# Rolling a matrix along its rows: the last quarter of the long copies in DMAs of one row per engine, with a window of DMAs in flight

## The chip, the cores and the metric

The kernel runs on one core of a Trainium2 chip. The metric is the device time of one execution in microseconds (us), lower is better; 2% either way counts as a change. Runs were made on several chips, and chips differ by over 1% on this kernel, so kernels are compared only with the runs of the kernel before on the same chip and in the same rounds. All runs here are at a granted clock of 1.0. A ratio is the mean time of one kernel's runs over that of the other's of the same rounds, so it is not quite the ratio of the medians that are quoted beside it.

## The reference

```python
x = np.random.randn(8192, 8192).astype(np.float32)   # 256 MiB
return np.roll(x, 100, axis=1)
```

Nothing is computed. Every byte has to be read once from HBM (the chip's main memory) and written once, 100 columns further right.

## The kernel before

`s` is 100, `a` is 128 and `g` is 28. The columns from 128 on (8,064 floats, 32,256 bytes of each row) are copied from HBM to HBM by DMAs on two rings (queues of DMAs), one issued by SP (`nc.sync`) and one by ACT (`nc.scalar`). The first 128 columns go through SBUF on GpSimd's own queue, with small VectorE copies. The outermost dimension `e` of a DMA has size 16, one value for each of the core's 16 DMA engines; the trace shows 16 increments of the semaphore for each DMA. A DMA has 512 row pieces, so 32 for each engine.

```python
engines = [nc.sync, nc.scalar]
xm = x.rearrange("(c e j) w -> j e c w", e=16, j=4)
om = out.rearrange("(c e j) w -> j e c w", e=16, j=4)
depth = n_rows // 64 // 4                     # 32 rows for each engine
for c in range(4):
    for j in range(4):
        cs = slice(c * depth, (c + 1) * depth)
        engines[j % 2].dma_start(out=om[j, :, cs, a:], in_=xm[j, :, cs, g:n_cols - s])
# ... (GpSimd loads both sides of the first 128 columns, VectorE joins them, GpSimd stores)
for k, h in enumerate(tiles):
    for q in range(Q):
        nc.gpsimd.dma_start(out=ot[k, q, :, :, :a], in_=h[:, q])
```

Of the kernel before, what the change touches and what calls it, by code (L numbers as in the profile page):

```python
# [1 line left out]

# [4 lines left out]


@with_exitstack
def kernel(  # L10
    ctx: ExitStack,
    tc: tile.TileContext,
    x: bass.AP,
    shift: int,
    out: bass.AP,
):
    nc = tc.nc
    n_rows, n_cols = x.shape
    s = shift % n_cols
    a = -(-s // 128) * 128  # L20
    g = a - s
    P = nc.NUM_PARTITIONS
    engines = [nc.sync, nc.scalar]
    n_chunks = 16
    rows = n_rows // n_chunks




    xm = x.rearrange("(c e j) w -> j e c w", e=16, j=4)  # L30
    om = out.rearrange("(c e j) w -> j e c w", e=16, j=4)
    depth = n_rows // 64 // 4
    for c in range(4):
        for j in range(4):
            if a < n_cols:
                cs = slice(c * depth, (c + 1) * depth)
                engines[j % 2].dma_start(out=om[j, :, cs, a:], in_=xm[j, :, cs, g:n_cols - s])
    if a == 0:
        return


    if a > 512:
        for i in range(n_chunks):
            r = slice(i * rows, (i + 1) * rows)
            nc.gpsimd.dma_start(out=out[r, :s], in_=x[r, n_cols - s:])
            if g > 0:
                nc.gpsimd.dma_start(out=out[r, s:a], in_=x[r, :g])
        return





    Q, J = 4, 8
    n_st = n_rows // (P * Q * J)
    reads = ctx.enter_context(tc.tile_pool(name="reads", bufs=n_st))
    heads = ctx.enter_context(tc.tile_pool(name="heads", bufs=n_st))
    xt = x.rearrange("(k p j q) c -> k q p j c", q=Q, j=J, p=P)
    ot = out.rearrange("(k p j q) c -> k q p j c", q=Q, j=J, p=P)
    tiles = []  # L60
    for k in range(n_st):
        t = reads.tile([P, Q - 1, J, a], x.dtype)
        h = heads.tile([P, Q, J, a], x.dtype)
        for q in range(1, Q):
            lead = bass.AP(tensor=x.tensor, offset=(k * P * J * Q + q) * n_cols - s,
                           ap=[[J * Q * n_cols, P], [Q * n_cols, J], [1, a]])
            nc.gpsimd.dma_start(out=t[:, q - 1], in_=lead)  # L67
        nc.gpsimd.dma_start(out=h[:, Q - 1, :, :s], in_=xt[k, Q - 1, :, :, n_cols - s:])  # L68
        nc.vector.tensor_copy(h[:, :Q - 1, :, :s], t[:, :, :, :s])  # L69
        if g > 0:  # L70
            nc.gpsimd.dma_start(out=h[:, 0, :, s:], in_=xt[k, 0, :, :, :g])  # L71
            nc.vector.tensor_copy(h[:, 1:, :, s:], t[:, :, :, s:])  # L72
        tiles.append(h)
    for k, h in enumerate(tiles):
        for q in range(Q):
            nc.gpsimd.dma_start(out=ot[k, q, :, :, :a], in_=h[:, q])  # L76


# [1 line left out]
_INS = ['x', 'shift']  # L80
_OUTS = [((8192, 8192), 'float32')]

_NUMBERS = {'shift': 100}


# [26 lines left out]
```

## Time and profile before

| what | value |
|---|---|
| time, six runs beside the changed kernel | 828.66 us median, 828.28 to 829.5 |
| run that was profiled (most likely on another, faster chip) | 817.2 us, span 815.4 us |
| bytes on the two rings, and on GpSimd's queue | 2 x 132.12 MB, 8.39 MB |
| data rate with the rings alone, 480 to 780 us | 332 GB/s copied, 664 GB/s of HBM traffic |
| last increments of SP's last DMA | first engine 755.8, last engine 813.3 us |

Read the profile from the data side: compute engines are idle, so the page's DMA lines and the table of windows (its last two columns: busy share of the 16 DMA engines, GB/s) tell nearly everything. The prediction below shows the lines.

### The profile page before, as it was taken

The numbers are of one execution on the slowest core, as the hardware profiler recorded it, in microseconds if no ns is written. First come the engines' busy times: TensorE is split into PE (matmuls) and PEld (weight loads), VectorE is DVE, ScalarE is ACT, GpSimd is POOL, SyncE is SP. The second block draws the span as 40 slices with busy tenths as digits, with TensorE's granted clock in tenths as the row PEclk, the third lists the DMA queues.
The fourth block names the chain that finished last, engine by engine and source line by source line (L and its number), as shares of the span: only waits on it lengthen the run. The fifth ranks groups of instructions, "written<-read, shape, count | busy, mean of one in ns | idle before, by whom it ended". The sixth has DMA issues, their size and how long they took to land. (4 is left out here: it accounts for less than half of the span.)

```text
span 815.4 us, 93 instructions
## 1 busy us (share of the span) xinstructions
DVE 3.7 (0%) x4; POOL 16.1 (2%) x22
## 2 busy tenths in 40 slices
DVE  0000000000000000000000000000000000000000
POOL 3000001000010000000000000000000000000000
DMA  9999999999999999999999999999999999999996
GB/s 310 341 328 347 330 349 335 337 340 346 338 337 346 338 348 348 347 333 345 340 344 337 349 326 335 334 329 334 335 329 331 329 335 334 332 331 332 329 334 250
DMA packets 10784, 272.63 MB, mean 334 GB/s; under 512 B 544, under 2 KB 544, under 8 KB 2592
## 3 DMA queue, kind: packets, MB, share of 16 engines
q10 hardware_dynamic: 4224, 132.12, 47.0%
q1 hardware_dynamic: 4224, 132.12, 46.9%
q0 software_dynamic: 2336, 8.39, 4.5%
HBM read 268.44 MB, written 268.44 MB: 658 GB/s over the span
## 5 line engine op out<-in xcount | busy, mean ns | idle before, releaser
L76 POOL DMA_DIRECT2D out_dram<-h x8 | 6.9, 954 | 170.1 <-DMA h<-in_x_dram 144.1
L67 POOL DMA_DIRECT2D t<-in_x_dram x6 | 5.4, 910 | 0.8 <-PEq L107 0.8
L69 DVE COPY h<-t 128x2400 f32<-128x2400 f32 x2 | 2.8, 1410 | 208.5 <-DMA t<-in_x_dram 208.5
L71 POOL DMA_DIRECT2D h<-in_x_dram x2 | 1.8, 883 | 28.6 <-DMA t<-in_x_dram 28.6
L68 POOL DMA_DIRECT2D h<-in_x_dram x2 | 1.8, 882 | 27.0 <-DMA t<-in_x_dram 27.0
L72 DVE COPY h<-t 128x672 f32<-128x672 f32 x2 | 1.0, 503 | 0.0
L93 POOL MEMSET const-float32-0.0<- 128x1 f32 x1 | 0.1, 99 | 0.2 <-issue 0.2
L93 POOL MEMSET const-bfloat16-1.0<- 128x1 bf16 x1 | 0.1, 103 | 0.0
L93 POOL MEMSET const-float32-1.0<- 128x1 f32 x1 | 0.1, 99 | 0.0
L93 POOL MEMSET const-uint8-127<- 128x1 uint8 x1 | 0.1, 99 | 0.0
## 6 DMA issues: line engine op xcount, KB each, us to landing
out_dram<-in_x_dram SPq DMA_DIRECT2D x8, 16128.0 KB, 401.3
out_dram<-in_x_dram ACTq DMA_DIRECT2D x8, 16128.0 KB, 400.5
out_dram<-h POOLq DMA_DIRECT2D x8, 512.0 KB, 182.5
t<-in_x_dram POOLq DMA_DIRECT2D x6, 512.0 KB, 118.2
h<-in_x_dram POOLq DMA_DIRECT2D x2, 400.0 KB, 151.3
h<-in_x_dram POOLq DMA_DIRECT2D x2, 112.0 KB, 146.1
```

Of the source, the lines that this page charges most:

```text
L67: nc.gpsimd.dma_start(out=t[:, q - 1], in_=lead)
L68: nc.gpsimd.dma_start(out=h[:, Q - 1, :, :s], in_=xt[k, Q - 1, :, :, n_cols - s:])
L69: nc.vector.tensor_copy(h[:, :Q - 1, :, :s], t[:, :, :, :s])
L71: nc.gpsimd.dma_start(out=h[:, 0, :, s:], in_=xt[k, 0, :, :, :g])
L72: nc.vector.tensor_copy(h[:, 1:, :, s:], t[:, :, :, s:])
L76: nc.gpsimd.dma_start(out=ot[k, q, :, :, :a], in_=h[:, q])
L93: nc = _bacc.Bacc("TRN2", target_bir_lowering=False, num_devices=1)
```

## The change

Its intent is to let the 16 DMA engines end together. Three quarters of the rows stay in DMAs of 32 rows per engine. The last quarter becomes 64 DMAs for each ring, of one row per engine. A ring issues the next of these only when an older one has landed, that is, when all 16 engines have added one to its semaphore (a counter that engines can wait on). At first 6 may be in flight on a ring, at the end 2. The framework's automatic waits do not allow that, so all DMAs move into a critical section (a stretch of code in which the kernel sets every wait itself) with semaphores of their own, and the GpSimd part is rewritten to match. The core of the diff (the rest rewrites the GpSimd part):

```diff
-    depth = n_rows // 64 // 4
-    for c in range(4):
-        for j in range(4):
-            ...
-                engines[j % 2].dma_start(out=om[j, :, cs, a:], in_=xm[j, :, cs, g:n_cols - s])
+    blocks = n_rows // 64
+    whole = blocks * 3 // 4
+    depth = 32
+    window = 6
...
+    with tc.tile_critical():
...
+        for q, ring in enumerate(rings):
+            bulk = nc.alloc_semaphore(f"bulk{q}")
+            slots = [nc.alloc_semaphore(f"slot{q}_{i}") for i in range(window)]
...
+                for c in range(0, whole, depth):
+                    for j in range(q, 4, 2):
+                        cs = slice(c, min(c + depth, whole))
+                        issue(ring, bulk, om[j, :, cs, a:], xm[j, :, cs, g:n_cols - s])
+                n, left, after = 0, 2 * (blocks - whole), []
+                for c in range(whole, blocks):
+                    for j in range(q, 4, 2):
+                        flying = max(2, window - n * (window - 1) // left)
+                        if n >= flying:
+                            ring.wait_ge(*after[n - flying])
+                        sem = slots[n % window]
+                        issue(ring, sem, om[j, :, c, a:], xm[j, :, c, g:n_cols - s])
+                        after.append((sem, expect[sem]))
+                        n += 1
```

More of the change, by code (lines that the diff above doesn't have):

```diff
@@ L22 @@
     P = nc.NUM_PARTITIONS
-    engines = [nc.sync, nc.scalar]
-    n_chunks = 16
-    rows = n_rows // n_chunks
+    rings = (nc.sync, nc.scalar)
     xm = x.rearrange("(c e j) w -> j e c w", e=16, j=4)
     om = out.rearrange("(c e j) w -> j e c w", e=16, j=4)
-    depth = n_rows // 64 // 4
-    for c in range(4):
-        for j in range(4):
-            if a < n_cols:
-                cs = slice(c * depth, (c + 1) * depth)
-                engines[j % 2].dma_start(out=om[j, :, cs, a:], in_=xm[j, :, cs, g:n_cols - s])
@@ L38 @@
-    if a == 0:
-        return
-    if a > 512:
-        for i in range(n_chunks):
-            r = slice(i * rows, (i + 1) * rows)
-            nc.gpsimd.dma_start(out=out[r, :s], in_=x[r, n_cols - s:])
-            if g > 0:
-                nc.gpsimd.dma_start(out=out[r, s:a], in_=x[r, :g])
-        return
-    Q, J = 4, 8
-    n_st = n_rows // (P * Q * J)
-    reads = ctx.enter_context(tc.tile_pool(name="reads", bufs=n_st))
-    heads = ctx.enter_context(tc.tile_pool(name="heads", bufs=n_st))
@@ L58 @@
-    xt = x.rearrange("(k p j q) c -> k q p j c", q=Q, j=J, p=P)
-    ot = out.rearrange("(k p j q) c -> k q p j c", q=Q, j=J, p=P)
-    tiles = []
-    for k in range(n_st):
-        t = reads.tile([P, Q - 1, J, a], x.dtype)
-        h = heads.tile([P, Q, J, a], x.dtype)
-        for q in range(1, Q):
-            lead = bass.AP(tensor=x.tensor, offset=(k * P * J * Q + q) * n_cols - s,
-                           ap=[[J * Q * n_cols, P], [Q * n_cols, J], [1, a]])
-            nc.gpsimd.dma_start(out=t[:, q - 1], in_=lead)
-        nc.gpsimd.dma_start(out=h[:, Q - 1, :, :s], in_=xt[k, Q - 1, :, :, n_cols - s:])
-        nc.vector.tensor_copy(h[:, :Q - 1, :, :s], t[:, :, :, :s])
-        if g > 0:
-            nc.gpsimd.dma_start(out=h[:, 0, :, s:], in_=xt[k, 0, :, :, :g])
-            nc.vector.tensor_copy(h[:, 1:, :, s:], t[:, :, :, s:])
-        tiles.append(h)
@@ L74 @@
-    for k, h in enumerate(tiles):
-        for q in range(Q):
-            nc.gpsimd.dma_start(out=ot[k, q, :, :, :a], in_=h[:, q])
+    blocks = n_rows // 64
+    whole = blocks * 3 // 4
+    depth = 32
+    window = 6
+    Q, J = 4, 8
+    narrow = 0 < a <= 512
+    n_st = n_rows // (P * Q * J) if narrow else 0
+    pool = ctx.enter_context(tc.tile_pool(name="heads", bufs=1))
+    reads = [pool.tile([P, Q - 1, J, a], x.dtype, name=f"reads{k}") for k in range(n_st)]
+    heads = [pool.tile([P, Q, J, a], x.dtype, name=f"heads{k}") for k in range(n_st)]
@@ new lines, with issue @@
+    with tc.tile_critical():
+        expect = {}
+        def issue(eng, sem, o, i):
+            eng.dma_start(out=o, in_=i).then_inc(sem, 16)
+            expect[sem] = expect.get(sem, 0) + 16
+        for q, ring in enumerate(rings):
+            bulk = nc.alloc_semaphore(f"bulk{q}")
+            slots = [nc.alloc_semaphore(f"slot{q}_{i}") for i in range(window)]
+            if a < n_cols:
+                for c in range(0, whole, depth):
[12 more added lines that the diff above has]
+                        n += 1
+            for sem in (bulk, *slots):
+                if sem in expect:
+                    ring.wait_ge(sem, expect[sem])
+        pooled = nc.gpsimd
+        paired = nc.alloc_semaphore("paired")
+        stored = nc.alloc_semaphore("stored")
+        xt = x.rearrange("(k p j q) c -> k q p j c", q=Q, j=J, p=P)
+        ot = out.rearrange("(k p j q) c -> k q p j c", q=Q, j=J, p=P)
+        n_pair = 0
+        for k in range(n_st):
+            t, h = reads[k], heads[k]
+            landed = nc.alloc_semaphore(f"landed{k}")
+            for q in range(1, Q):
+                lead = bass.AP(tensor=x.tensor, offset=(k * P * J * Q + q) * n_cols - s,
+                               ap=[[J * Q * n_cols, P], [Q * n_cols, J], [1, a]])
+                issue(pooled, landed, t[:, q - 1], lead)
+            issue(pooled, landed, h[:, Q - 1, :, :s], xt[k, Q - 1, :, :, n_cols - s:])
+            if g > 0:
+                issue(pooled, landed, h[:, 0, :, s:], xt[k, 0, :, :, :g])
+            nc.vector.wait_ge(landed, expect[landed])
+            nc.vector.tensor_copy(h[:, :Q - 1, :, :s], t[:, :, :, :s]).then_inc(paired, 1)
+            n_pair += 1
+            if g > 0:
+                nc.vector.tensor_copy(h[:, 1:, :, s:], t[:, :, :, s:]).then_inc(paired, 1)
+                n_pair += 1
+        per = n_pair // n_st if n_st else 0
+        for k in range(n_st):
+            pooled.wait_ge(paired, (k + 1) * per)
+            for q in range(Q):
+                issue(pooled, stored, ot[k, q, :, :, :a], heads[k][:, q])
+        if a > 0 and not narrow:
+            for r in range(0, n_rows, 512):
+                issue(pooled, stored, out[r:r + 512, :s], x[r:r + 512, n_cols - s:])
+                if g > 0:
+                    issue(pooled, stored, out[r:r + 512, s:a], x[r:r + 512, :g])
+        if stored in expect:
+            pooled.wait_ge(stored, expect[stored])
```

## The prediction

> **What bounds the kernel now.** I read the page of the kernel before first, for who is busy at all, then the table of windows, for how the data rate changes with time, and last the ring's waits and the times of the single semaphore increments in the trace.
>
> ```profile
> span 815.4 us, 93 instructions
> ...
> DVE 3.7 (0%) x4; POOL 16.1 (2%) x22
> ...
> DMA  9999999999999999999999999999999999999996
> ...
> q10 hardware_dynamic: 4224, 132.12, 47.0%
> q1 hardware_dynamic: 4224, 132.12, 46.9%
> q0 software_dynamic: 2336, 8.39, 4.5%
> HBM read 268.44 MB, written 268.44 MB: 658 GB/s over the span
> ...
> out_dram<-in_x_dram SPq DMA_DIRECT2D x8, 16128.0 KB, 401.3
> ```
>
> The compute engines do nothing that counts. The DMA engines are nine tenths busy or more in every slice but the last. Two rings (q1 and q10, issued by ACT and SP) move the long row pieces from HBM to HBM, one packet of 32,256 bytes for each row piece (4,096 on each ring, the other 128 packets being semaphore writes), and the GpSimd queue q0 moves the first 128 columns through SBUF. All of it adds up to 658 GB/s of HBM traffic.
>
> ```profile
> 100.00:200.00 100.00, 0.00 (x0) 3.46 (x4) 1.00 1.00 340
> 200.00:440.00 240.00, 1.83 (x2) 3.47 (x4) 1.00 1.00 342
> 480.00:620.00 140.00, 0.00 (x0) 0.00 (x0) 1.00 1.00 332
> 620.00:780.00 160.00, 0.00 (x0) 0.00 (x0) 1.00 0.99 332
> 780.00:790.00 10.00, 0.00 (x0) 0.00 (x0) 1.00 0.95 342
> 790.00:800.00 10.00, 0.00 (x0) 0.00 (x0) 1.00 0.88 319
> 800.00:805.00 5.00, 0.00 (x0) 0.00 (x0) 1.00 0.79 323
> 805.00:810.00 5.00, 0.00 (x0) 0.00 (x0) 1.00 0.66 284
> 810.00:815.40 5.40, 0.00 (x0) 0.00 (x0) 1.00 0.22 96
> ```
>
> In this table of windows the last two columns are the busy share of the 16 DMA engines and the GB/s moved. The fall from 342 to 332 is not a loss. The GpSimd queue's last transfer lands at 462.8 us, so its 8.39 MB ran at 18 GB/s beside some 324 of the rings. A ring byte is read and written in HBM, a GpSimd byte touches HBM once: 2 x 324 + 18 = 666 GB/s before, 2 x 332 = 664 after. So HBM traffic is flat at about 665 GB/s from 100 to 790 us, whatever the mix. That flat rate is the bound. A single engine is not at its own limit meanwhile: in the packet records a row piece takes 1.55 us between 520 and 700 us, but exactly 1.194 us (27.0 GB/s) when others have stopped. At 27 GB/s each, 332 / 27 = 12.3 busy engines are enough to fill the shared rate. From 780 to 800 us with only some 14.8 busy it still held; only after 800 us does it drop.
>
> The last pair of bulk DMAs shows the uneven ends. The sixteen increments of SP's last DMA come at 755.8, 795.9, 799.6, 801.1 and then twelve times between 807.2 and 813.3 us; ACT's last is at 814.4. One engine is done 57 us early, three more about 15 us early, the rest within 6 us.
>
> **What the Trainium skill says.** "HBM Reference", section "Specifications", gives about 716 GB/s for an HBM domain; the 665 measured here is 93% of it, so the trace agrees that one core's DRAM-to-DRAM copy is held by HBM and not by how it is issued. "DMA: Bandwidth & Descriptors", section "Why a DMA increments its semaphore by 16 and not by 1": each engine that takes part counts separately and only the full 16 means landed, so a wait on a DMA is a wait for its slowest engine. The sixteen separate increments above agree. The same section wants one semaphore for each in-flight slot, and the new kernel has six for each ring. Section "Measured" of that page advises DMAs of 1 MiB or more; the new ones carry 16 x 32,256 bytes = 504 KiB. Its table is of loads issued from GpSimd, and the trace before has no ring DMA under 16 MB, so no run here shows that penalty yet.
>
> **The change, part by part.** (1) The GpSimd part is rewritten with explicit semaphores but issues the same 18 transfers in the same queue; loads go out a little earlier (before, two of them waited for a free semaphore until 35 and 65 us), but the queue behind them was never empty, and everything lands by 463 us of 815. Worth 0. (2) The first three quarters are the same 16 MB DMAs, six for each ring. The waits for a semaphore before the fifth to eighth are gone.
>
> ```profile
> SPq L37 <- DMA out_dram<-in_x_dram: 47.6, 4, 16.7
> ```
>
> Those 47.6 us of waits on SP cost no data time, as three more DMAs lay in the ring each time and the DMA share stayed at 1.00. Worth 0. (3) The last quarter, 1,024 row pieces for each ring from about 617 us (when the sixth DMA lands now), becomes 64 DMAs of 16 rows, one row on each engine. Bytes and packet size are unchanged; per ring 62 more sets of 16 semaphore writes, at 9 ns each by the packet records: 62 x 2 x 9 ns = 1.1 us of an engine's time in all, beside other engines' work under the HBM bound, so about 0. Issue time: 64 x 0.65 us (shortest ring issues in the trace are 0.61 and 0.67) = 42 us for each ring, spread over 195 us, hidden. (4) The window: by the code's formula 13 DMAs are issued with 6 in flight, then 13 with 5, 13 with 4, 13 with 3, 12 with 2. Work is not moved between engines: row e of 16 still goes to the same engine. What the window does is hold the early engines back, to at most 12 rows (two rings of 6) ahead of the slowest, then 4.
>
> **What evening out can be worth.** The window from 780 us to the end moves 10.16 MB. At 332 GB/s that is 30.6 us; half of the 16 packets in flight at 780 add 0.26 MB or 0.8 us. Perfectly even engines would end their data at 780 + 31.4 = 811.4 us. The last packet really ends at 814.1. So the uneven end costs **2.7 us**, not the 57 us of the first engine, because the others take over the bandwidth that it leaves. With 2 rows on each ring at the end some unevenness stays, about one packet, 1 us. Gain: 1.5 to 2 us.
>
> **What the window can cost.** At 332 GB/s both rings together finish a 16-row DMA of 0.516 MB every 1.55 us, so one ring every 3.1 us. With 2 in flight, issue to landing may take 6.2 us before the rate falls. From the trace: wake-up 0.05 us (landing at 105.8, next issue at 105.86), first issue at 0.74 to first packet at 2.17 = 1.43 us, last packet end to landing 0.3 us, so 1.8 us without data; a row of its own and one of the other ring ahead of it, 2 x 1.55 = 3.1. Sum 4.9 us against 6.2. It fits, with less than one packet of slack, and packets vary from 1.19 to 1.87 us (10th and 90th percentile), so the last 12 DMAs (37 us) may lose 2 to 3% or 1 us. With 3 or more in flight (9.3 us and up) nothing. Added waits at the end and the critical section: an estimate of 0.3 us. Sum: -1.5 to -2, +1 and +0.3, which is near nothing. I lean half a microsecond further to the gain, as a depth that falls from 6 to 2 looks like one that was tried out. Point: **827.5 us**, 1.3 under 828.8.
>
> **The rivals.** *Starvation:* the loaded round trip is longer than 4.9 us. If it were 8 us, the last 12 would come every 4 us in place of 3.1, +11 us (about 839); if 6.5 us, +2. For it: the 4.9 has little slack, and each DMA waits for the slowest of 16. Against it: 12.3 busy engines of 16 fill HBM, so a few starved ones cost nothing. *Lockstep:* held close together, all 16 engines go through HBM in the same order. The kernel before is in that state at its start, and there
>
> ```profile
> 20.00:60.00 40.00, 0.00 (x0) 0.88 (x1) 1.00 0.99 331
> ```
>
> shows 331 where later windows with the same queues show 340: 2.6% less. Over 195 us that would be +5 us (about 832.5). *Better order:* the tail in step with shallow queues could instead raise the HBM rate; 2% over 195 us would be -4 us (about 823.5). The 342 GB/s of 780 to 790 us, with an engine or two fewer, is the only hint. *Hidden anyway:* the window only keeps idle those engines that would have idled at the end, and the time is the same to 0.5 us (828.5).
>
> **Range and chances.** A change of over 2% means 16.6 us, 8% of the last quarter. The uneven end holds 2.7 us in all, and 665 GB/s is a bound that no issue order changed by more than some 3% in this trace, so faster by 2% gets 0.03. Slower by 2% needs the long round trip: 0.04. The range 822.5 to 832.5 holds lockstep at one end and better order at the other.
>
> **What would show it.** Right: GB/s near 332 in the windows of the last quarter until some 5 us before the end, the increments of the last DMA within 3 us of each other, a span 1 to 2 us shorter, and SP waiting long in its ring without the DMA share falling before the last 40 us. Starvation shows as a DMA share and GB/s that sink in steps as the depth goes 4, 3, 2; lockstep as a share near 1.00 with packets over 1.55 us and fewer GB/s; better order as GB/s over 340 in the last quarter. The prediction is wrong if the last quarter's rate moves by over 3%.

## The result, and the profile after

The changed kernel took 831.71 us median (828.46 to 832.34, six runs) against 828.66 us: a ratio of 1.003, with a 95% interval of 1.0013 to 1.0047. It is slower by 0.3%, which is clear of noise and far inside the 2% that would count.

The two first profiles must not be subtracted. The profile of before spans 815.4 us and that of the changed kernel 830.5 us, 15 us apart, while the timed runs are 3 us apart. Most likely the first profile was taken on a faster chip than the first timed runs: on other chips the unchanged kernel itself later took 818.4 us and 829.3 us. The page of the changed kernel, in the lines that answer to those of before:

```profile
span 830.5 us, 225 instructions
...
q10 hardware_dynamic: 5216, 132.13, 47.5%
q1 hardware_dynamic: 5216, 132.13, 46.3%
...
HBM read 268.44 MB, written 268.44 MB: 646 GB/s over the span
...
out_dram<-in_x_dram SPq DMA_DIRECT2D x6, 16128.0 KB, 370.8
...
out_dram<-in_x_dram SPq DMA_DIRECT2D x64, 504.0 KB, 12.3
```

(q1 is SP's ring and q10 ACT's: here ACT issues first, and the first packet is on q10. The prediction names them the other way round; none of its numbers depends on it.) Packets on each ring rose from 4,224 to 5,216: 62 more DMAs of 16 semaphore writes each, as predicted. The bytes are the same. A small DMA takes 12.3 us from issue to landing in the median, over all depths. The table of windows of the same run (last two columns: busy share of the DMA engines, GB/s):

```profile
480.00:600.00 120.00, 0.00 (x0) 0.00 (x0) 1.00 1.00 328
620.00:700.00 80.00, 0.00 (x0) 0.00 (x0) 1.00 0.98 329
700.00:780.00 80.00, 0.00 (x0) 0.00 (x0) 1.00 0.99 329
780.00:790.00 10.00, 0.00 (x0) 0.00 (x0) 1.00 0.96 313
790.00:800.00 10.00, 0.00 (x0) 0.00 (x0) 1.00 0.85 297
800.00:805.00 5.00, 0.00 (x0) 0.00 (x0) 1.00 0.61 206
805.00:810.00 5.00, 0.00 (x0) 0.00 (x0) 1.00 0.97 348
810.00:820.00 10.00, 0.00 (x0) 0.00 (x0) 1.00 0.94 329
820.00:830.50 10.50, 0.00 (x0) 0.00 (x0) 1.00 0.55 186
```

From 480 to 600 us the code is still the old bulk, and the rate is 328 where the first profile of before had 332. Most likely that is the chip. From 620 to 780 us, at depths 6 to 3, the rate stays at 329: the window costs nothing there. From about 786 us the schedule allows 2 in flight, and the rate sags to 297 and then 206 GB/s, where the kernel before had still 319 and 323. In the packet records of that stretch one row takes 3.08 us (797.02 to 800.10 us) where most others take 1.2 to 2.1. The next two DMAs land at 801.6 and 801.8 us: their sixteenth increments come 4.2 and 2.8 us after the fifteenth, and both rings wait for them before they issue again. The packet records name no engine; that it is one engine, and the one with the slow row, is read from these times.

SP's waits, from the list of who waited for whom on SP's queue, answer to the 47.6 us of before:

```profile
SPq L47 <- DMA out_dram<-in_x_dram: 338.0, 58, 179.2
...
SPq L43 <- POOLq L43: 0.4, 1, 0.4
```

The ring now waits 58 times. Most of the 338 us are harmless, since other DMAs lie in the ring meanwhile. The last line is new too: SP waits for GpSimd at the exit of the critical section.

### The profile page after: what moved, and what is told of

Its sections match the earlier page's. It is cut to its first block, busy times and chain, and to the rows that moved or that the text cites. A ratio compares the mean times of both kernels' runs of the same rounds, so it can differ in the third digit from the quotient of the medians.

```text
span 830.5 us, 225 instructions
## 1 busy us (share of the span) xinstructions
DVE 3.7 (0%) x4; POOL 16.1 (2%) x22
## 3 DMA queue, kind: packets, MB, share of 16 engines
q10 hardware_dynamic: 5216, 132.13, 47.5%
q1 hardware_dynamic: 5216, 132.13, 46.3%
## 5 line engine op out<-in xcount | busy, mean ns | idle before, releaser
L47 POOL DMA_DIRECT2D out_dram<-heads x8 | 7.0, 1007 | 233.3 <-DVE heads L98 233.3
L47 POOL DMA_DIRECT2D reads<-in_x_dram x6 | 5.4, 909 | 1.1 <-PEq L142 1.1
L95 DVE COPY heads<-reads 128x2400 f32<-128x2400 f32 x2 | 2.8, 1411 | 243.2 <-DMA heads<-in_x_dram 243.2
L47 POOL DMA_DIRECT2D heads<-in_x_dram x4 | 3.5, 882 | 0.0
## 6 DMA issues: line engine op xcount, KB each, us to landing
out_dram<-in_x_dram ACTq DMA_DIRECT2D x64, 504.0 KB, 12.3
out_dram<-in_x_dram SPq DMA_DIRECT2D x64, 504.0 KB, 12.3
```

Source lines behind the costliest of these rows:

```text
L47: eng.dma_start(out=o, in_=i).then_inc(sem, 16)
L95: nc.vector.tensor_copy(h[:, :Q - 1, :, :s], t[:, :, :, :s]).then_inc(paired, 1)
```

## The experiments

Twelve runs were made, in four calls. Each call used one chip, so that its ratios share the runs of before: the first call 818.39 us median (817.77 to 819.54), the second 829.33 us (825.66 to 832.1), the third 818.42 us (817.7 to 820.42), the last 819.99 us (817.13 to 822.6). All results were correct.

My theory was that depth 2 starves the engines. The rivals were that small DMAs cost as such, that any window lowers the HBM rate, and that the new form has a fixed cost.

### The kernel before, profiled again (first call)

No edit.

> The kernel before, unchanged, for a second profile of it. Its first profile spans 815.4 us (run 817.2) while its six timed runs lie at 828.3 to 829.5, so that profile caught an execution 11 us faster than the timed ones, whereas the profile of the changed kernel (832.2) is one of its timed runs. All theories: ratio 1.000 (0.999 to 1.001). If the first profile was a lucky execution, this one spans about 827 us and its bulk is slower throughout (sixth DMA of SP landing near 627 us in place of 617); if profiling itself speeds it up, it spans 815 again.

It took 819.32 us (ratio 1.0007, 0.9994 to 1.002), with a profiled span of 817.5 us. Its other timed runs and its profiled run agree (818.17 to 819.47 us). So neither expectation was quite met: profiling speeds nothing up, and no lucky execution is needed either, if the first profile came from a chip of this speed and the first timing from a slower one. That is the likeliest reading, though the chip of the first profile is not recorded.

### The changed kernel again (first call)

No edit.

> The changed kernel, unchanged, as the yardstick on this chip. All theories: 830 to 832 us, ratio 1.002 to 1.005 as before. If starvation at depth 2 is the cause, its last 12 DMAs of each ring should again show stretches where one late packet on one engine leaves the others idle (211 GB/s from 800 to 805 us in the first profile), perhaps at other times.

820.25 us, ratio 1.0024 (1.0012 to 1.0037): the loss repeats on another chip, at 2.0 us. Its rate from 780 to 810 us was 313 to 316 GB/s against 333 from 480 to 600; a hole as deep as that of the first profile does not show in these 10 us windows. (The 211 GB/s of the expectation is 206 in the table above.)

### No window (first call)

```diff
-                        if n >= flying:
-                            ring.wait_ge(*after[n - flying])
```

> The 64 DMAs of one row on each engine stay, all waits between them are taken out, so that the ring alone limits them. Theory starvation (my first choice): the loss is gone, 828 to 829 us, ratio 0.999 to 1.001, and engines end as unevenly as before (one engine some 30 to 50 us early). Rival small DMAs (splitting, issue and semaphore writes cost): as slow as the changed kernel, ratio 1.003. Rival fixed cost (critical section, GpSimd part, waits at the end): also 1.003.

819.66 us (818.18 to 823.41), ratio 1.0021 (1.0004 to 1.0038). I expected the loss to be gone. It was not, or not all of it: something else was left. The fixed cost of the next experiment is about as large as this loss. Nor did the engines end as unevenly as before: the increments of the last DMAs are spread over 14 us (SP) and 15 us (ACT), not 57.

### Bulk alone in the new form (first call)

```diff
-    whole = blocks * 3 // 4
+    whole = blocks
```

> All of the rings' work in DMAs of 32 rows per engine as before, but in the new form with its critical section, its own semaphores and its GpSimd part. Theory starvation: ratio 1.000, 828.5 us. Rival small DMAs: 1.000 too. Rival fixed cost: 1.003, 831 us, with the loss showing before the first ring packet or after the last landing.

819.44 us, ratio 1.0007 (0.9995 to 1.0019), too little to tell from nothing by time. The trace shows the fixed cost directly, though. The first ring packet starts at 2.38 us in place of 2.17, and the span ends 2.17 us after the last landing, in place of 0.94 in the kernel before on the same chip. With the small DMAs in the critical section (nine traces, of the changed kernel and its variants, without the last run) it is 2.40 to 2.43 us and 2.37 to 2.39 us. So the fixed cost is about 0.25 + 1.4 = 1.7 us, not the 0.3 that I had put down for it.

### Six in flight to the end (second call)

```diff
-                        flying = max(2, window - n * (window - 1) // left)
+                        flying = window
```

> Six in flight on each ring to the end. Theory starvation at depth 2: the loss goes, ratio 0.998 to 1.001 (827 to 829 us), last increments spread over some 10 us. Rival lockstep (any window that holds the engines close lowers the HBM rate): ratio still about 1.002 to 1.003. Rival fixed cost or small DMAs: 1.003.

830.58 us, ratio 1.0019 (0.9996 to 1.0043). This is what the fixed cost alone makes (1.7 of 829 us is 1.002), but the interval also holds zero. The sixteen increments of a DMA are spread over 11 us at the end (the mean of its last eleven DMAs), so a window of 6 evens the engines little. Its rate in the windowed quarter is the bulk's (329 GB/s from 480 to 600 us and 328 to 329 from 600 to 798 us, worked out from the packet records), which speaks against a window lowering the HBM rate.

### Two in flight through the whole last quarter (second call)

```diff
-                        flying = max(2, window - n * (window - 1) // left)
+                        flying = 2
```

> Two in flight on each ring through the whole last quarter, five times as many DMAs at depth 2 as in the changed kernel (62 against 12 for each ring). Theory starvation: five times the loss of about 3 us, so 840 to 845 us, ratio 1.015 to 1.02, with GB/s of 300 to 315 throughout the last quarter in place of 330. Rivals lockstep, fixed cost, small DMAs: no more than 1.005.

838.68 us (837.92 to 845.78), ratio 1.0147 (1.0109 to 1.0186): 12 us slower than before by the means and 9.4 by the medians, as two of the six runs took 845.78. This is a little under the 840 to 845 us that I wrote, with the ratio just at the lower edge, and far over the 1.005 that the rivals allowed. Depth 2 costs time, and more of it costs more.

```profile
620.00:700.00 80.00, 0.00 (x0) 0.00 (x0) 1.00 0.88 304
700.00:780.00 80.00, 0.00 (x0) 0.00 (x0) 1.00 0.95 317
```

In the first trace of the changed kernel, on a chip of about the same speed, both windows stand at 329 GB/s.

### Never below three (second call)

```diff
-                        flying = max(2, window - n * (window - 1) // left)
+                        flying = max(3, window - n * (window - 1) // left)
```

> The same schedule but never below 3 in flight. Theory starvation: nearly all of the loss gone, ratio 0.999 to 1.001. Rivals: 1.003. If depth 3 already starves (9.3 us at the shared rate against a round trip of 5 to 7), something in between.

828.5 us, ratio 0.9994 (0.9973 to 1.0015). With one character changed no loss shows, but the interval was wide and the changed kernel was not on this chip. So both ran together next.

### The changed kernel and the floor of three on one chip (third call)

> The changed kernel once more, as yardstick beside the next three on the same chip. All theories: ratio 1.002 to 1.004. My account by now: about +1.5 us fixed (the critical section lets the first ring DMA go 0.2 us later and its exit adds some 1.2 us, chiefly a drain of 1.1 us on GpSimd, as the traces of the bulk-only and of the changed kernel show), about +2 us of starvation at depth 2, and 1 to 2 us won back by evener ends.

> Never below 3 in flight, again, with the changed kernel on the same chip this time, as its first interval (0.9973 to 1.0015) was wide. My account (the starvation at depth 2 taken away, the fixed cost and the evener ends kept): 1 to 2.5 us faster than the changed kernel, ratio to before 0.999 to 1.001. Rival fixed cost alone: the same as the changed kernel to 0.5 us.

The changed kernel took 821.74 us (820.62 to 822.64), ratio 1.0041 (1.0028 to 1.0054). With floor 3 it took 818.34 us (817.61 to 819.04), ratio 0.9998 (0.9984 to 1.0011). The difference of the means is 3.4 us, and the runs do not overlap. I had expected 1 to 2.5 us. Windows of the changed kernel's trace here:

```profile
780.00:790.00 10.00, 0.00 (x0) 0.00 (x0) 1.00 0.79 290
790.00:800.00 10.00, 0.00 (x0) 0.00 (x0) 1.00 0.92 313
800.00:810.00 10.00, 0.00 (x0) 0.00 (x0) 1.00 0.87 310
```

and of the trace with floor 3:

```profile
780.00:790.00 10.00, 0.00 (x0) 0.00 (x0) 1.00 1.03 339
790.00:800.00 10.00, 0.00 (x0) 0.00 (x0) 1.00 0.98 332
800.00:810.00 10.00, 0.00 (x0) 0.00 (x0) 1.00 0.98 313
```

Before 780 us they differ by at most 4 GB/s either way. The loss is in the stretch with depth 2. Over the last DMAs of each ring (number 52 to 63, the ones that the two schedules treat differently) the semaphore records give:

| kernel | mean issue to landing, SP and ACT, us | time between landings, SP and ACT, us |
|---|---|---|
| changed, 2 in flight | 6.9 and 6.8 | 3.21 and 3.52 |
| floor 3, 3 in flight | 9.2 and 9.3 | 2.94 and 3.10 |

At 333 GB/s a ring's share allows one landing every 3.1 us. The intervals of the changed kernel are longer than those with floor 3 by 0.35 us in the mean; eleven of them make 3.8 us, which is about the measured 3.4. The first column is no second proof: a ring at its depth issues when a DMA lands, so the trip is about the depth times the interval. The loss varies: in the trace of the changed kernel of the first call the intervals are only 3.02 and 3.30 us.

How the engines idle matters more than how much. From the packet records, the number of rows in transfer at an instant, which stands for the number of engines at work (now and then it passes 16, so it is not exact):

| trace, stretch in us | mean rows | time with 4 or fewer | time with 13 or more |
|---|---|---|---|
| before, 780 to 805 | 14.3 | 0% | 87% |
| changed (third call), 785 to 814 | 14.3 | 4% | 85% |
| changed (first profile), 785 to 825 | 13.9 | 6% | 86% |
| floor 3 (third call), 780 to 810 | 15.9 | 0% | 100% |

The mean is the same in the first two rows. In the kernel before, a few engines are finished and the rest keep HBM nearly full. In the changed kernel, for about one twentieth of the time almost all stand still together, while one to four late rows finish. This accounts for the rate: the prediction's rule, 27 GB/s for each row in transfer and never more than 332, taken at every instant, gives 331, 311, 306 and 332 GB/s for the four rows of the table; measured (each row's bytes spread over its time) are 330, 313, 301 and 330.

### Small DMAs in the kernel before, without a critical section (third call)

```diff
-    for c in range(4):
+    cuts = [0, 32, 64, 96] + list(range(97, n_rows // 64 + 1))
+    for lo, hi in zip(cuts, cuts[1:]):
         for j in range(4):
...
-                cs = slice(c * depth, (c + 1) * depth)
+                cs = slice(lo, hi)
```

> The kernel before with only its loop changed: six DMAs of 32 rows and 64 of one row for each ring, left to the framework, whose four semaphores for each ring hold it to 4 in flight to the end; no critical section, GpSimd part as before. My account (evener ends without fixed cost and without depth 2): 1 to 2 us faster than before, ratio 0.9975 to 0.999, with the first ring packet at 2.2 us and the span ending 1.0 us after the last landing as before. Rival small DMAs: ratio 1.001 to 1.003 though nothing else was changed. Rival hidden anyway (evening out is worth nothing): 1.000.

818.64 us, ratio 1.0003 (0.999 to 1.0016). The framework itself holds each ring to 4 in flight. I had expected 0.9975 to 0.999; the gain did not appear. The first packet starts at 2.21 us, but the exit takes 1.62 us after the last landing in place of 0.94, as SP's last wait for a DMA's semaphore ends 0.75 us after the last landing, in place of 0.10, so the expectation of 1.0 us was wrong too. What is shown: 504 KiB DMAs as such cost nothing that can be measured here, and evening out the engines with 4 in flight is worth at most about 1.5 us (the lower end of the interval, -0.8 us, and the 0.7 us of extra exit).

### One in flight (third call)

```diff
-                        flying = max(2, window - n * (window - 1) // left)
+                        flying = 1
```

> One in flight on each ring through the last quarter: the period of a ring's DMA is then its whole round trip. Starvation with the round trip of 4.9 us that the prediction summed up: 63 DMAs at 4.9 in place of 3.1 us, +113 us, about 930 to 945 us. With less queueing, as only one row of the other ring can lie ahead and an engine alone needs 1.2 us for a row: 1.8 + 1.2 to 2.4, so 3.0 to 4.2 us and +10 to +70 us. Rivals in which depth does not matter: within 5 us of the changed kernel.

922.03 us (two runs), ratio 1.1267: 104 us slower. The first of the two expectations (+113 us) was close, the second (+10 to +70 us) too low. Its DMA issues from 650 to 900 us (last column: median us from issue to landing):

```profile
out_dram<-in_x_dram SPq DMA_DIRECT2D x53, 504.0 KB, 4.7
out_dram<-in_x_dram ACTq DMA_DIRECT2D x52, 504.0 KB, 4.7
```

This is the round trip itself, with one row of the other ring beside it: 4.7 us, of which by the prediction's sum 1.8 are without data. The rate is 219 GB/s from 700 to 900 us. That is less than idle engines alone explain: the rule of 27 GB/s for each row in transfer, up to 332, would give 293, and a row takes 1.76 us in the mean where the bulk of before has 1.55. Why rows are slower at depth 1 stays open.

### Floor three and an early drain (last call)

```diff
         if stored in expect:
             pooled.wait_ge(stored, expect[stored])
+            pooled.drain()
```

> Never below 3 in flight, and GpSimd does a drain of its own inside the critical section, at some 467 us when its queue has landed, so that the drain at the section's exit finds nothing to do. My account of the fixed cost: the exit's GpSimd drain shrinks from 1.13 us to under 0.2, the span ends some 1.4 us after the last landing in place of 2.4, and the time is about 1 us under the kernel with floor 3, so ratio 0.998 to 0.9995. Rival (the exit drain takes its 1.1 us whatever came before): ratio 0.999 to 1.001 as with floor 3 alone and the drain still at 1.1 us.

820.34 us, ratio 1.0003 (0.9981 to 1.0025) on a chip with a wider scatter. By time nothing is resolved. The trace is clear. The drain of GpSimd at the exit of the critical section, without the edit (floor 3, third call; ns shortest/median/longest, then start):

```profile
L43 POOLq DRAIN  x1: 1130/1130/1130, 815.3 to 815.3; - x1
```

and with it:

```profile
L43 POOLq DRAIN  x1: 34/34/34, 816.4 to 816.4; - x1
```

The drain did shrink from 1.13 us to 0.03, yet the exit only fell from 2.39 to 2.02 us, not to the 1.4 that I expected: SP's own chain of drains and semaphores through the exit, which ran beside GpSimd's drain, then sets the end (its NOP comes 1.20 us after the last landing, and came 1.57 us after it, just behind GpSimd's drain, without the edit). This version was meant to beat both kernels. It does not, within what these runs can tell.

## Why the prediction was right or wrong

The range (822.5 to 832.5 us) and the class (within 2%) held. In part that was luck: the range was made wide for lockstep and better order, and neither came. The point, 827.5 us, was on the wrong side of 828.66: the change loses about 2.5 us (0.3% of 828.7) where I had put a gain of 1.3. Two terms of the sum were too small, the cost of depth 2 and the fixed cost. Half a microsecond more came from the lean to the gain, which rested on no number. The mechanisms named were the right ones.

- **The bound.** Right as far as the runs tell. HBM traffic stays flat, and no schedule with three or more in flight moved its rate: 331 to 332 GB/s in the windows from 620 to 780 us with floor 3 and with the kernel before on chips of the same speed.
- **GpSimd part, removed semaphore waits, issue time, semaphore writes.** Right as far as the runs tell. Bulk alone in the new form is at 1.0007, and the small DMAs alone at 1.0003. An issue takes 0.51 us (not 0.65) and stays hidden.
- **Lockstep and better order.** Neither is seen with three to six in flight; rates there stay within 1.5% of those of the bulk.
- **What evening out is worth.** About right, by the traces. The ends did come closer: the increments of the last DMAs of the changed kernel lie within 1.6 us (SP) and 1.9 us (ACT), as predicted. And the prediction's own sum can be done for every kept trace: the time from 780 us to the end of the last row, less the time that the bytes left at 780 us take at that trace's rate from 480 to 600 us. (For before it gives 2.9 us where the prediction had 2.7, as rows that are under way at 780 us are counted in part here and were estimated there.)

| traces | lost at the end, us |
|---|---|
| bulk DMAs to the end (before, before again, bulk alone) | 2.9, 2.8, 3.1 |
| floor 3 (second, third and last call) | 0.4, 1.1, 1.1 |
| 4 in flight by the framework; six in flight; no window | 1.9; 2.5; 2.3 |
| changed kernel (first profile, first call, third call) | 3.9, 1.9, 4.8 |

  So floor 3 wins back about 2 us, which its fixed cost of 1.7 us uses up; that agrees with its standing level with before. The small DMAs without the critical section win back 1.0 us, of which their longer exit takes 0.7.
- **What depth 2 costs: the first step that failed.** The prediction said "the last 12 DMAs (37 us) may lose 2 to 3% or 1 us". They lost 3.4 us on one chip, about 2.5 us by comparing the ratios 1.0024 and 0.9994 of two chips, and 2.7 us in the mean by the last row of the table less the row of floor 3. The mechanism was named and the single round trip well summed (4.9 us, measured 4.7 at depth 1). But the sum used mean row times, and a DMA lands with the slowest of 16 engines. In the third call's trace of the changed kernel the ninth of the sixteen increments came 4.1 (SP) and 5.0 us (ACT) after the issue in the mean of the last twelve DMAs, as summed and inside the 6.2 us allowed; the sixteenth came after 6.9 and 6.8 us. The argument against the rival, that "12.3 busy engines of 16 fill HBM, so a few starved ones cost nothing", holds for engines that idle one by one, as in the kernel before. A window of two makes them idle all at once.
- **The fixed cost: the second step that failed.** Put at 0.3 us as an estimate; it measured 1.7 us in the traces, 0.25 at the start and 1.4 at the exit. For the bulk alone the trace has 1.4 us, where the times show 0.6 with an interval that ends at 1.6.

In sum, for the three traces of the changed kernel: +1.7 fixed, and what is lost at the end against the 2.9 of before (+1.0, -1.0 and +1.9), which makes +2.7, +0.7 and +3.6 us. The times beside them are +2.5, +2.0 and +3.4 us; a trace is a single execution, so they need not agree closely.

What stays open: why one row is late (the one of 3.08 us), why the loss at the end of the changed kernel varies from 1.9 to 4.8 us from trace to trace, and why chips differ in HBM rate (328 against 333 GB/s).

## What to carry to other kernels

When a shared memory is the bound, the last engine's lateness costs only what the others cannot take over: compute that area under the falling rate first (2.7 us here, not 57), before building anything to remove it. A window over DMAs that each wait for all 16 engines needs to cover the round trip of the slowest engine, not of the mean one; three in flight on each of two rings were enough here and two were not. Look at the exit of a new synchronisation form in the trace, as its fixed cost can be as large as the gain.

## What the Trainium skill lacked or had wrong

- "DMA: Bandwidth & Descriptors", section "Measured", advises DMAs of 1 MiB or more. For these HBM-to-HBM copies, size did not matter while enough were in flight: 504 KiB DMAs ran at 331 to 336 GB/s with 4 in flight on each ring (ratio to 16 MB DMAs 1.0003). The section does not give the depth needed: one on each ring gave 219 GB/s, two 304 to 317, three 332 to 339 (780 to 800 us).
- The same page, section "Why a DMA increments its semaphore by 16 and not by 1", says what a full count means, and the traces agree. It does not warn that a shallow window then idles all engines together: up to 6% of the time with 4 or fewer rows in transfer.
- "HBM Reference", section "Specifications", gives one figure for a domain. Here 656 to 665 GB/s of traffic was reached, depending on the chip, and the same kernel took 818.4 us on one and 829.3 us on another. I found no page that tells of such differences between chips.
- I found no page that gives the cost of leaving a critical section after GpSimd DMAs: its drain took 1.13 us, or 0.03 us when one had been done before, and the whole exit 2.4 us against 0.95.
